# One streaming-encoder layer: the mixers' weight tiles from a written plan, their roundings in emission order, new charges of the emission clock, modulation at another pace

## The chip, the core and the metric

The kernel runs on one core of a Trainium2 chip. The metric is the device time of one execution in microseconds. Engines are named as the profile names them: PE is TensorE (PEld its weight loads), DVE VectorE, ACT ScalarE, POOL GpSimd, SP SyncE, which issues most of the DMAs.

## What is computed

One layer of a hybrid encoder, 512 prompt tokens and 64 sample tokens, model width 2048, all in float32. Cut to what matters:

```python
mod = jax.nn.silu(c) @ w_ada + b_ada                     # modulation: sh1, sc1, g1, sh2, sc2, g2
h = rmsnorm(x, norm1) * (1 + sc1) + sh1
proj = h @ w_in                                          # columns: a_q a_k a_v a_r a_lr | b_q b_k b_v b_g b_beta b_alpha
# group A: gated linear attention, 4 heads (GLA), state 128 x 256
# group B: gated delta rule after a causal convolution, 8 heads (GDN), state 128 x 128
out = concat([o_a, o_b]) @ w_out
x = x + g1 * out
h = rmsnorm(x, norm2) * (1 + sc2) + sh2
f = (silu(causal_dwconv(h @ w_up_gate) + b) * (h @ w_up_val)) @ w_down
y = rmsnorm(x + g2 * f, final_norm)
```

Prompt and sample have a modulation and recurrent states each; the new states are outputs too.

## The kernel before

A GEMM tile is 128 output columns for all 576 tokens, as two halves of 288. Precision is kept by splitting each float32 operand into a rounded part and a rest: ScalarE copies the raw weights (`raw`) to the rounded `wh`, VectorE subtracts and writes the rest `wl`. One product of 128 contraction rows (`mm6`) is six matmuls, three terms for two halves: `wh` by `hh`, `wh` by `hl`, `wl` by `hh` (lines 744 and 746). A weight tile holds 8 such products (512 KB); an input tile of the projection takes two weight tiles.

The stages in order: the head (normalisation, first modulation, and six input tiles, whose results partly go to DRAM as `early`), the mixers, the output projection in two halves (first the contraction over the GDN heads, then over the GLA heads), the FFN up and down, the final norm.

In the mixers PE gets one long stream: `gdn_heads` and `gla_heads` emit the input tiles, and between the products the recurrences of heads that have their inputs are emitted as jobs, written as generators. After each product `tick` advances an emission clock (`now`, 0.795 us a product), lets every short task go one step, lets the first job in the list that can go on take one step, and lets the modulation take steps: a VectorE multiply-add of a 128 x 512 block of `w_ada` into `acc`, 512 of them in all, at `ADA_RATE` steps a tick and only while the clock's VectorE is not more than 1 us behind.

The clock also foresees when a job's result is ready. Every operation of a wrapped engine is charged with a duration (`OP_US`) to that engine's free time and to the job's `chain`; `until` holds the generator back until the clock has reached the chain. Operations that go through the wrappers `tv`, `ta`, `jv`, `ja` are bound to issue in emission order on VectorE and ScalarE. Not bound are the weight roundings: `split` emits the load and both roundings at the start of each weight tile with priority and with `floating` set, so that they issue as far ahead as buffers allow (three buffers for `raw`, three for `wh` and `wl`).

Job operands live in a pool of 29 tiles of 128 x 512 (`_MixPool`). A job asks for room with `room(n)` and waits until `n + SPARE` tiles are free. The sample jobs (`gdn_samples`, `gla_samples`) process all heads' 64 sample tokens at once and run behind the others. Head outputs go to DRAM (`od`), and `load_o` brings them back, alternately through the buffers `xr` and `raw`, and splits them for the output projection; those of the GDN heads before its first half, those of the GLA heads before its second. Small matmuls and transposes of the jobs are issued in the wrappers of lines 2410 and 2414; line 2368 issues job operations of VectorE and ScalarE, line 2395 other wrapped operations.

Of the kernel before, what the change touches and what calls it, by code (L numbers as in the profile page):

```python
# [32 lines left out]
SPARE = 5  # L33
JOB_RATE, ADA_RATE = 1.0, 0.72
# [3 lines left out]
TABLE_US, COLUMN_US = 1.28, 0.06  # L38
# [76 lines left out]
class Kern:  # L115
    def __init__(self, tc, ctx, i, o):
        self.tc, self.nc, self.ctx, self.i, self.o = tc, tc.nc, ctx, i, o
        self.n = 0
        self.cp = ctx.enter_context(tc.tile_pool(name="cp", bufs=1, side="left"))
        self.psum = ctx.enter_context(ExitStack())  # L120
        self.pg = self.psum.enter_context(tc.tile_pool(name="pg", bufs=2, space=PSUM))
        self.c, self.scrap = {}, []
# [91 lines left out]
    def gdn(self, qF, kF, x, gain, hcols, gb, s0, s_out, o_put, last_level, room=None):  # L214
# [15 lines left out]
        nbe, wk, egl = self.g_nbe[:, hcols], self.g_wk[:, hcols], self.g_egl[:, hcols]  # L230
        yield from self.wait_for(x, "q")
        yield from self.wait_for(x, "k")
        back, room = room, room or (yield from self.room(5))
# [5 lines left out]
        A.activation(du, du, AF.Exp, scale=-1.0)  # L239
        for m, op, up in ((du, ALU.is_ge, 1), (dl, ALU.is_gt, -1)):  # L240
            for z, sign in ((slice(0, 2), up), (slice(2, 4), -up)):
                self.pool.affine_select(m[:, z], m[:, z], pattern=[[0, 2], [sign, P]], compare_op=op, fill=0.0, base=0, channel_multiplier=-sign)
        if pair:
            self.pool.memset(du[0:64, 0:2, 64:P], 0.0)
            self.pool.memset(du[64:P, 2:4, 0:64], 0.0)
        A.activation(gb, gb, AF.Exp)
# [13 lines left out]
        V.scalar_tensor_tensor(kt[:, 1], kt[:, 1], -1.0, beta, op0=ALU.mult, op1=ALU.mult)  # L260
        yield from self.until()
# [64 lines left out]
        for b in range(4):  # L326
# [16 lines left out]
            yield from self.hop()  # L343
            for n, (lo, hi, s_) in enumerate(parts):
# [18 lines left out]
            A.activation(ops[:, b], ps[:, :P], AF.Copy, scale=rq[:, at:at + 1])  # L363
# [73 lines left out]

    def timed(self, f, *a):
# [26 lines left out]
    def inverse16(self, a, work, room):  # L465
# [23 lines left out]
        for i in range(1, 15):  # L489
# [3 lines left out]
            V.tensor_tensor(xx[:, rest, :i], xx[:, rest, :i], xt[:, rest, :i], op=ALU.add)  # L493
            if i % 4 == 0:
# [26 lines left out]
    def gla(self, nb, qF, kF, g, x, s0, s_out, o_put, room=None):  # L521
# [12 lines left out]
        back, room = room, room or (yield from self.room(4))  # L534
# [8 lines left out]
        for s in LEVELS:  # L543
# [10 lines left out]
            V.tensor_tensor(qe, asks(g), ref, op=ALU.subtract)  # L554
            A.activation(e, e, AF.Exp, scale=1.0 / 16.0)
# [5 lines left out]
            for r in range(nb // 2):  # L561
# [22 lines left out]
        self.drop(kF, back)  # L584
        egl = self.small(4)
        A.activation(egl[:, :nseg].rearrange("p (h n) -> p h n", h=2), walk(g, seg - 1, (hw - seg + 1, 2), (seg, nseg // 2)),
                     AF.Exp, scale=1.0 / 16.0)
# [12 lines left out]
        for b in range(nb):  # L600
# [7 lines left out]
            if not first:  # L608
                for lo, hi, s_ in parts:
                    T.matmul(ops[lo:hi, b % 2], qd[:, at_b, lo:hi], s_, start=False, stop=True)  # L610
            for n, (lo, hi, s_) in enumerate(parts):
# [12 lines left out]
            A.activation(junk, ops[:, b % 2], AF.Square, scale=1.0 / 16.0, accum_out=ss[:, b:b + 1])  # L624
# [123 lines left out]
    def gemm(self, ps, src, acts, order=None, tick=lambda: None, w=None):  # L748
# [612 lines left out]
    def in_tile(self, off, order=None):  # L1361
        ps = self.pgt()
        self.gemm(ps, self.w_in(off), self.h, order, tick=self.tick)
        return ps

    def slots(self, t):

        v = t.rearrange("p (two r t) -> p two r t", two=2, t=P)
        return v[:, 0], v[:, 1, :, ::-1]

# [23 lines left out]
    def gdn_conv(self, ps, t, dst, name, h, done):  # L1394
# [8 lines left out]
        V.tensor_copy(cb[:, 518:582].rearrange("p (h t) -> p h t", h=2), ps[:, :, HP:HT])  # L1403
        V.tensor_copy(cb[:, 515:518], self.vmap["st_conv"].rearrange("p (i t) -> p t i", i=3)[:, t])
# [31 lines left out]
    def gdn_heads(self):  # L1436
# [3 lines left out]
        def conv_tile(n, off, h, x):  # L1440
            ps = self.ps_q0 if h == 0 and n == 0 else self.in_tile(off + h * P)
# [4 lines left out]
        def qk(h):  # L1446
            x = {}
            q = conv_tile(0, OFF_BQ, h, x)
            if h == 0:
                self.narrow(self.kp)  # L1450
            gb = self.decays(self.gd[4 * h:4 * h + 4])
            k = conv_tile(1, OFF_BK, h, x)
            self.start(self.gdn(q, k, x, self.vec("gdn_norm", 0), slice(4 * h, 4 * h + 4),
                                      gb, None, o["p_gdn"][0, 0, h],
# [3 lines left out]
        def vg(h, x):  # L1458
            conv_tile(2, OFF_BV, h, x)
            ps = self.in_tile(OFF_BG + h * P)  # L1460
# [23 lines left out]
    def gdn_samples(self):  # L1484
# [4 lines left out]
        for name, n in (("v", "v"), ("gate", "g")):  # L1489
# [5 lines left out]
                          self.vec("gdn_norm", 0), slice(32, 36), self.decays(self.gd[32:36], room), _States(self, "state_gdn", P),  # L1495
# [9 lines left out]
    def gla_samples(self, x):  # L1505
# [3 lines left out]
        self.put_ready(x, "g", None, 0.0)  # L1509
        yield from self.gla(2, *tiles, x,  # L1510
# [11 lines left out]
    def gla_gate(self, h, g, done):  # L1522

        V, A, T = self.tv, self.ta, self.jt
        y, gss, ys = self.m(), self.half()[:, :TS], self.half()[:, :TS]
# [24 lines left out]
        done(self.chain + HOP_US)  # L1550

    def gla_heads(self):
# [3 lines left out]
        for h in range(4):  # L1556
            self.ending = h == 3
            qk, x = [], {}
            for name, off, sc in (("aq", OFF_AQ, Q_SCALE), ("ak", OFF_AK, 1.0)):
                if (name, h) in self.early:  # L1560
                    t = self.m()
                    self.nc.sync.dma_start(t, self.early[name, h])
                    qk.append(b4(t))
                    continue
                ps = self.in_tile(off + h * P)
# [4 lines left out]
            g = b4(self.m())  # L1570

            def gated(at, x=x, h=h):
                self.put_ready(x, "g", None, at)
                if h == 3:
                    self.start(self.gla_samples(xs))
            self.spawn(self.gla_gate(h, g.rearrange("p b t -> p (b t)"), gated))
            self.start(self.gla(4, *qk, g, x, None, o["p_gla"][0, 0, h], lambda f, t, h=h: self.put_o(2 * h + f, t)))
            vT = [self.m().rearrange("p (b t) -> p b t", b=2) for _ in range(2)]
            for f in range(2):
                ps = self.in_tile(OFF_AV + h * 256 + f * P)  # L1580
# [4 lines left out]
                def turn(t=t, f=f, vT=vT, x=x, h=h):  # L1585
                    tp = self.transpose4(b4(t))
                    self.drop(t)
                    for b in range(2):
# [6 lines left out]
            for f in range(2):  # L1595

                ps = self.in_tile(OFF_AR + h * 256 + f * P, (8, 0) if h == 3 and f == 1 else None)
# [666 lines left out]
def layer_kernel(tc, i, o):  # L2264
    nc = tc.nc
    with ExitStack() as ctx:
# [18 lines left out]
        with ExitStack() as early:  # L2285
            K.wp = pool(early, "wp", "right", bufs=3)
            with ExitStack() as right:
# [9 lines left out]
                with ExitStack() as st:  # L2297
# [6 lines left out]
                    K.ada = K.ada_blocks(range(8, 24), acc)  # L2304
                    K.gdn_heads()
                    K.gla_heads()

                    w, ob = {}, []
                    for k in range(8, 16):
                        ob.append(K.load_o(k, lambda k=k: K.htiles(k)))  # L2310
                        if k == 11:
                            w[0] = K.wtile(K.w_cols("w_out", 0, 8)(0, 8))
                    K.x1 = []
                    for m in range(KD):
# [3 lines left out]
                        K.gemm(ps, K.w_cols("w_out", m, 8), ob, tick=K.tick, w=w.get(m))  # L2318
# [191 lines left out]
```

## Time and profile before

| | us |
|---|---|
| median of 3 runs | 2729.12 (2728.79 to 2731.55) |
| the profiled execution | 2729.87 |
| its span, first to last instruction | 2728.2 |
| PE busy in the span | 2682.6 (98%) |
| DVE busy | 2292.2 (84%) |
| ACT busy | 1295.6 (47%) |
| POOL busy | 477.8 (18%) |

In the profile's rows a group is named by line, engine, operation and tiles (out<-in). Its busy time and the mean of one follow, then the engine's idle time ahead of it and what ended that. A wait row names who waited for whom, the sum, the number and the longest. Matmuls overlap, so that a busy PE is not a measure of its rate.

### The profile page before, as it was taken

What the parts mean: (1) busy time and instruction counts of PE and PEld (TensorE: products, weight loads), DVE (VectorE), ACT (ScalarE), POOL (GpSimd) and SP (SyncE); (2) the same over time, 40 slices, a digit from 0 to 9 for tenths busy, and PEclk for the clock granted to TensorE, in tenths of its full rate; (3) what the DMA queues carried; (4) which work ended last, traced back from release to release, by engine and by line L of the source; (5) the groups of instructions that cost most, each with busy time, mean ns of one, the idle gap of its engine ahead of it and who ended that gap; (6) DMA issues with size and microseconds to landing.
All of it is one profiled execution on the core that took longest, in us unless ns stands there. A gap on an engine that the chain in (4) does not pass through costs nothing.

```text
span 2728.2 us, 52233 instructions
## 1 busy us (share of the span) xinstructions
PE 2682.6 (98%) x20208; PEld 2620.1 (96%) x20208; DVE 2292.2 (84%) x3747; ACT 1295.6 (47%) x2317; POOL 477.8 (18%) x461
## 2 busy tenths in 40 slices
PE   7999999999999999999999999999999999999998
PEld 5799999999999999999999999999999999999998
DVE  4579899988989895688999999999999976888996
ACT  4246454555554442554545454545454544333453
POOL 0001010110001000001333333333333300000241
PEclk9999999999999999999999999999999999999999
DMA  9986565555565583634555555555555595674762
GB/s 303 347 256 186 151 171 161 168 171 147 154 180 164 159 270 90 179 98 120 162 168 163 167 163 167 165 165 167 163 168 162 165 312 184 197 223 121 237 181 82
DMA packets 646203, 487.84 MB, mean 179 GB/s; under 512 B 66601, under 2 KB 568356, under 8 KB 645956
## 3 DMA queue, kind: packets, MB, share of 16 engines
q1 hardware_dynamic: 632852, 471.04, 57.5%
q10 hardware_dynamic: 13104, 13.47, 1.7%
q8 instruction: 159, 2.61, 0.4%
q14 instruction: 88, 0.72, 0.1%
HBM read 400.38 MB, written 84.04 MB: 178 GB/s over the span
## 4 chain that ended last, share of the span: by engine, by line
PE 82%; DVE 8%; DMA 4%; issue 3%; ACT 2%; SPq 0%; POOL 0%; ACTq 0%; DVEq 0%; POOLq 0%
PE g L744 17%; PE bank L1881 16%; PE bank L1880 16%; PE bank L1882 16%; PE g L746 8%; PE bank L2414 4%; DVE wl L1790 2%; PE bank L744 1%; PE bank L2410 1%; DVE m L2368 1%; DVE wl L2395 1%; DMA raw<-in_w_out_dram 1%; PE bank L973 1%; DMA raw<-in_w_in_dram 1%; DVE slot L2076 1%
## 5 line engine op out<-in xcount | busy, mean ns | idle before, releaser
L1881 PE MATMUL bank<-slot,wh 128*128 128x290 f32 (+1 forms) x3584 | 1067.3, 298 | 0.0
L1880 PE MATMUL bank<-slot,wh 128*128 128x290 f32 (+1 forms) x3584 | 1063.1, 297 | 1.0 <-DVE v L1903 0.6
L1882 PE MATMUL bank<-slot,wl 128*128 128x290 f32 (+1 forms) x3584 | 1060.3, 296 | 1.3 <-DVE wl L1790 1.2
L1882 PEld LDWEIGHTS bank<-slot,wl 128*128 128x128 f32 x3584 | 680.0, 190 | 2.9 <-DVE wl L1790 2.5
L1880 PEld LDWEIGHTS bank<-slot,wh 128*128 128x128 f32 x3584 | 675.4, 188 | 5.2 <-issue 4.4
L1881 PEld LDWEIGHTS bank<-slot,wh 128*128 128x128 f32 x3584 | 677.0, 189 | 0.1
L744 PE MATMUL g<-hh,wh 128*128 128x288 f32 x2048 | 470.1, 310 | 1.6 <-DVE kt L2395 0.7
L1788 ACT ACTIVATE wh<-raw 128x1024 fp32r<-128x1024 f32 (+1 forms) x304 | 280.7, 924 | 348.5 <-PE bank L1881 325.2
L746 PE MATMUL g<-hh,wl 128*128 128x288 f32 x2048 | 442.7, 297 | 2.3 <-DVE wl L1141 2.3
L744 PE MATMUL g<-hl,wh 128*128 128x288 f32 x2048 | 442.8, 297 | 0.3 <-DVE hl L775 0.2
L1790 DVE TENSOR_TENSOR wl<-raw,wh 128x1024 fp32r<-128x1024 f32 (+1 forms) x304 | 374.2, 1231 | 69.0 <-ACT wh L1788 66.0
L1788 ACT ACTIVATE wh<-s 128x1024 fp32r<-128x1024 f32 (+1 forms) x228 | 211.0, 927 | 296.5 <-PE bank L1881 136.6
L744 PEld LDWEIGHTS g<-hh,wh 128*128 128x128 f32 x2048 | 325.5, 189 | 15.9 <-issue 10.4
L746 PEld LDWEIGHTS g<-hh,wl 128*128 128x128 f32 x2048 | 330.8, 189 | 4.2 <-DVE wl L1141 2.7
L744 PEld LDWEIGHTS g<-hl,wh 128*128 128x128 f32 x2048 | 330.6, 189 | 2.7 <-issue 1.9
L1790 DVE TENSOR_TENSOR wl<-s,wh 128x1024 fp32r<-128x1024 f32 (+1 forms) x228 | 251.0, 1102 | 13.7 <-ACT wh L1788 12.5
L2395 ACT ACTIVATE wh<-raw 128x1024 fp32r<-128x1024 f32 x135 | 143.1, 1062 | 185.6 <-PE g L744 145.1
L2004 POOL TENSOR_TENSOR j<-j,j 128x288 f32<-128x288 f32 (+1 forms) x120 | 186.0, 1557 | 84.0 <-ACT j L2008 82.1
L2395 DVE TENSOR_TENSOR wl<-raw,wh 128x1024 fp32r<-128x1024 f32 x135 | 165.9, 1229 | 35.5 <-ACT wh L2395 35.2
L2395 DVE SCALAR_TENSOR_TENSOR acc<-aw,ct,acc 128x512 f32<-128x512 f32 x264 | 187.7, 743 | 0.0
L2395 DVE SCALAR_TENSOR_TENSOR acc<-xr,ct,acc 128x512 f32<-128x512 f32 x216 | 154.2, 748 | 0.0
L2076 DVE TENSOR_TENSOR slot<-bank,slot 128x288 f32<-128x288 f32 x184 | 83.0, 451 | 33.7 <-PE bank L1882 32.6
(317 smaller groups left out, 3269.4 us busy)
## 6 DMA issues: line engine op xcount, KB each, us to landing
raw<-in_w_up_dram SPq DMA_DIRECT2D x176, 512.0 KB
raw<-in_w_in_dram SPq DMA_DIRECT2D x100, 512.0 KB
raw<-in_w_down_dram SPq DMA_DIRECT2D x128, 320.0 KB
slot<-cd SPq DMA_DIRECT2D x140, 288.0 KB
aw<-in_w_ada_dram SPq DMA_DIRECT2D x74, 512.0 KB
cd<-j SPq DMA_DIRECT2D x120, 288.0 KB
xr<-in_w_ada_dram SPq DMA_DIRECT2D x54, 512.0 KB
hraw<-in_w_ada_dram SPq DMA_DIRECT2D x40, 512.0 KB
```

What stands on the lines that cost most here:

```text
L744: T.matmul(ps[:, h if bank is None else bank, :n], wh, x[:, h, :n], start=f, stop=False)
L746: T.matmul(ps[:, h if bank is None else bank, :n], wl, ah[:, h, :n], start=False, stop=stop)
L973: T.matmul(ps[32 * k:32 * k + 32, :w], cs[:, k0 + k], got[n][k // per][:, k % per], start=(n == together - 1 + 8 * g + 4 * (1 - mi)), stop ...
L1788: self.nc.scalar.activation(hi, src, AF.Copy)
L1790: self.nc.vector.tensor_tensor(lo, src, hi.bitcast(F32), op=ALU.subtract)
L1880: T.matmul(ps, wh[:, j], hi, start=(c < 3 and j == 0), stop=False, skip_group_check=True)
L1881: T.matmul(ps, wh[:, j], lo, start=False, stop=False, skip_group_check=True)
L1882: T.matmul(ps, wl[:, j], hi, start=False, stop=(j == n - 1), skip_group_check=True)
L2004: minus = lambda out, a, b: G.tensor_tensor(out, a, b, op=ALU.subtract)
L2076: V.tensor_tensor(dst, ps, dst, op=ALU.add)
L2395: r = f(*a, **kw)
L2414: return self.engine.matmul(out, *a, **kw)
```

## The change

- The mixers' weight tiles come from a list written beforehand (`make_plan`): all 100 weight tiles of the remaining input tiles, then 16 of the output projection's first half. Three loads are issued at once; after that `gemm_planned` issues one load per weight tile.
- The roundings are no longer floating. The ScalarE rounding of the next weight tile is emitted after the second product of the current one (`w_split`), the VectorE rounding once the clock says that the first is done, or after the sixth product (`w_rest`). Both are bound in emission order.
- The clock: `beside` charges an operation that nothing of the job waits for next without lengthening the job's chain; small steps of the 16 x 16 inversion are charged 0.12 us more per pair; waits (`until`) stand ahead of some ScalarE operations.
- Rooms are granted in the order of asking, except that `gla_gate` asks in front and without spare; `SPARE` goes from 5 to 2. Decays, early q and k, the gate and the turned v take their tiles later. `gla_samples` waits until the last GLA head has begun.
- `ADA_RATE` goes from 0.72 to 0.58 steps a tick.

```diff
-SPARE = 5
-JOB_RATE, ADA_RATE = 1.0, 0.72
+SPARE = 2
+JOB_RATE, ADA_RATE = 1.0, 0.58
...
-    def room(self, n):
-        while self.mp.spare() < n + SPARE:
+    def room(self, n, first=False):
+        room = _Room(n)
+        self.asking.insert(0 if first else len(self.asking), room)
+        while self.asking[0] is not room or self.mp.spare() < n + (0 if first else SPARE):
             yield WAIT
+        self.asking.pop(0)
         self.mp.held += n
-        return _Room(n)
+        return room
...
+    @contextmanager
+    def beside(self, at):
+        old, self.chain = self.chain, max(at, self.now)
+        yield
+        self.chain = max(old, self.chain)
...
             V.tensor_tensor(xx[:, rest, :i], xx[:, rest, :i], xt[:, rest, :i], op=ALU.add)
+            self.slower("V", 2 * SMALL_US)
...
-            A.activation(ops[:, b], ps[:, :P], AF.Copy, scale=rq[:, at:at + 1])
+            with self.beside(ready):
+                A.activation(ops[:, b], ps[:, :P], AF.Copy, scale=rq[:, at:at + 1])
...
+    def gemm_planned(self, ps, acts, order):
         n, i = len(acts), 0
-        for k0 in order or range(0, n, 8):
-            k1 = min(n, k0 + 8)
-            wh, wl = w or self.wtile(src(k0, k1))
-            for k in range(k0, k1):
+        for k0 in order:
+            if not self.ready:
+                self.w_split()
+            self.w_rest()
+            wh, wl = self.ready.pop(0)
+            for k in range(k0, k0 + 8):
                 self.mm6(ps, wh[:, k - k0], wl[:, k - k0], acts[k], i == 0, i == n - 1)
-                tick()
+                self.tick()
+                if k == k0 + 1:
+                    self.w_split()
+                    self.w_load()
+                elif self.rest and (self.now >= self.rest[3] + HOP_US or k == k0 + 5):
+                    self.w_rest()
                 i += 1
+    def w_load(self):
+        if self.plan:
+            raw, src = self.raw(), self.plan.pop(0)
+            with self.tc.high_priority(offset=AHEAD):
+                self.nc.sync.dma_start(raw.rearrange("p (k n) -> p k n", k=8), src)
+            self.loaded.append(raw)
+    def w_split(self):
+        if not self.loaded:
+            return
+        raw = self.loaded.pop(0)
+        hi, lo = [self.wq.tile([P, 1024], F32R, tag="w" + c, bufs=3, name=self.name("w" + c)) for c in "hl"]
+        self.ready.append([x.rearrange("p (k n) -> p k n", k=8) for x in (hi, lo)])
+        old, self.chain = self.chain, self.now
+        self.ja.activation(hi, raw, AF.Copy)
+        self.rest, self.chain = (raw, hi, lo, self.chain), old
+    def w_rest(self):
+        if self.rest:
+            raw, hi, lo, at = self.rest
+            old, self.chain, self.rest = self.chain, at, None
+            self.jv.tensor_tensor(lo, raw, hi.bitcast(F32), op=ALU.subtract)
+            self.chain = old
+    def make_plan(self):
+        off = [OFF_BK]
+        for h in range(8):
+            off += [OFF_BQ + (h + 1) * P, OFF_BK + (h + 1) * P] if h < 7 else []
+            off += [OFF_BV + h * P, OFF_BG + h * P]
+        for h in range(4):
+            off += [o + h * P for n, o in (("aq", OFF_AQ), ("ak", OFF_AK)) if (n, h) not in self.early]
+            off += [o + h * 256 + f * P for o in (OFF_AV, OFF_AR) for f in range(2)]
+        self.plan = [self.w_in(o)(k0, k0 + 8) for n, o in enumerate(off) for k0 in ((8, 0) if n == len(off) - 1 else (0, 8))]
+        self.plan += [self.w_cols("w_out", m, 8)(0, 8) for m in range(KD)]
+        self.loaded, self.ready, self.rest = [], [], None
+        for _ in range(3):
+            self.w_load()
...
-    def gla_samples(self, x):
+    def gla_samples(self, x, last):
+        while "begun" not in last:
+            yield WAIT
         room = yield from self.room(7)
...
+                    K.make_plan()
                     K.gdn_heads()
                     K.gla_heads()
-                    w, ob = {}, []
+                    ob = []
                     for k in range(8, 16):
                         ob.append(K.load_o(k, lambda k=k: K.htiles(k)))
-                        if k == 11:
-                            w[0] = K.wtile(K.w_cols("w_out", 0, 8)(0, 8))
...
-                        K.gemm(ps, K.w_cols("w_out", m, 8), ob, tick=K.tick, w=w.get(m))
+                        K.gemm_planned(ps, ob, (0,))
```

More of the change, by code (lines that the diff above doesn't have):

```diff
@@ L230, in gdn @@
         nbe, wk, egl = self.g_nbe[:, hcols], self.g_wk[:, hcols], self.g_egl[:, hcols]
+        back, room = room, room or (yield from self.room(6))
+        gb = self.decays(self.gd[hcols], room)
+        self.moved()
         yield from self.wait_for(x, "q")
         yield from self.wait_for(x, "k")
-        back, room = room, room or (yield from self.room(5))
+        yield from self.until()
         dl, du = self.m4(room), self.m4(room)
@@ L533, in gla @@
         yield from self.wait_for(x, "g")
-        back, room = room, room or (yield from self.room(4))
+        g = x["g"]()
+        kept = [type(t) is tuple for t in (qF, kF)]
+        back, room = room, room or (yield from self.room(3 + sum(kept)))
+        x["begun"] = True
+        if any(kept):
+            qF, kF = [self.get_early(t, room) if type(t) is tuple else t for t in (qF, kF)]
+            self.moved(sum(kept))
+            yield from self.until()
         at = self.m(room)[:, :w].rearrange("p (b t) -> p b t", b=nb)
@@ L554, in gla @@
             V.tensor_tensor(qe, asks(g), ref, op=ALU.subtract)
+            yield from self.until()
             A.activation(e, e, AF.Exp, scale=1.0 / 16.0)
@@ L1587, in turn @@
                     self.drop(t)
+                    if f == 0:
+                        vT += [self.m().rearrange("p (b t) -> p b t", b=2) for _ in range(2)]
                     for b in range(2):
```

100 lines of the change are left out of this document (57 added, 43 removed).

## The prediction

> **What bounds the kernel now.** I read the page first: the span and the share of each engine. Then the busy time by stage, cut where the mixers begin and end.
>
> ```profile
> span 2728.2 us, 52233 instructions
> PE 2682.6 (98%) x20208; PEld 2620.1 (96%) x20208; DVE 2292.2 (84%) x3747; ACT 1295.6 (47%) x2317; POOL 477.8 (18%) x461
> 140.00:960.00 820.00, 813.74 (x6270) 793.06 (x6270) 724.04 (x1578) 419.72 (x1018) 69.47 (x72) 1.00 0.61 173
> 960.00:1101.00 141.00, 138.24 (x1009) 133.53 (x1008) 101.81 (x203) 55.54 (x99) 7.05 (x21) 0.99 0.60 180
> ```
>
> The columns of the last two rows are the stretch, its length, the busy time of PE, weight loads, DVE, ACT and POOL, the granted TensorE clock, the DMA share and GB/s. TensorE is busy 98% of the span. The change touches what is emitted between 140 and 1101 us (input projection, both mixers, first half of the output projection), and there PE stands idle for 6.3 + 2.8 = 9.0 us in all. No matmul is added or removed, so the gain is bounded by stalls of about this size. Next, who ends PE's and the weight loads' waits there (engine, line waited for, us in total, times, longest), and the same for ACT and DVE from 200 to 1000 us:
>
> ```profile
> PE bank L2414 <- DVE m L2368: 3.1, 4, 1.0
> PE bank L2414 <- ACT m L2395: 2.0, 1, 2.0
> PE bank L2414 <- DVE m L2395: 1.7, 3, 1.0
> PE bank L2414 <- DVE sq L2368: 1.4, 2, 0.9
> PE g L744 <- DVE kt L2395: 0.7, 1, 0.7
> PEld bank L2414 <- issue: 7.7, 23, 1.2
> ACT wh L2395 <- PE g L744: 121.2, 53, 6.6
> DVE wl L2395 <- ACT wh L2395: 15.2, 14, 3.5
> ```
>
> All five PE rows, 8.9 us, are waits of or behind the recurrence jobs' small matmuls (bank, line 2414), four of them on VectorE and one on ScalarE. No row has PE waiting for a rounded weight (wl, wh): the GEMM itself is fed in time. The last two rows show what today's roundings do: issued as far ahead as buffers allow, they sit on ScalarE waiting for a buffer that PE still holds, and on VectorE waiting for ScalarE, with job work behind them.
>
> **The change part by part.** Sums are made against the profiled execution's 2729.87 us (span 2728.2 and 1.7 around it), 0.75 above the runs' median of 2729.12.
>
> *Roundings in emission order and the clock's charges.* The 116 weight tiles of the plan (the 100 halves of input tiles in the row below, and 16 of the output projection) keep their one ScalarE and one VectorE rounding each; only the place moves. Now a rounding can land in front of a job operation that a PE matmul needs:
>
> ```profile
> raw<-in_w_in_dram SPq DMA_DIRECT2D x100, 512.0 KB
> 369.33 1.21 DVE L2395 TENSOR_TENSOR wl<-raw,wh 128x1024 fp32r<-128x1024 f32 x1
> ...
> 372.05 1.22 DVE L2395 TENSOR_TENSOR wl<-raw,wh 128x1024 fp32r<-128x1024 f32 x1
> ...
> 375.60 0.34 DVE L2368 SCALAR_TENSOR_TENSOR sq<-bank,kt,m 128x128 f32<-128x128 f32 x1
> 376.09 0.46 PE L2414 MATMUL bank<-sq,m 128*128 128x128 f32 x2 [0.44 <-DVE sq L2368]
> ```
>
> Two roundings, started 2.7 us apart, then a job operation late by 0.44 us. Not every such stall has one before it:
>
> ```profile
> 403.90 2.54 DVE L2395 SCALAR_TENSOR_TENSOR ca<-conv_in,cols,ca 128x579 f32<-128x579 f32 x3 [0.26 <-ACT ca L2395]
> 406.42 1.09 DVE L2395 TENSOR_TENSOR m<-cm,consts 128x128 f32<-128x128 f32 x3
> 407.56 0.71 PE L2414 MATMUL bank<-m,m 128*128 128x128 f32 x4 [0.41 <-DVE m L2395]
> ```
>
> Here only convolution steps stand ahead. The PE rows without the 2.0 on ScalarE and the 0.77 at 964.72 us (both below) make 6.1 us. In order, and charged where it stands, a rounding is foreseen by the emission clock; its prices of convolution and modulation steps stay too low. So I take half gone: −3.1 (bounds: all gone, −6.1; as much again added, +6.1). Of the 7.7 us in which a weight load was late with no releaser shown, most overlaps a running matmul; I take a quarter, −2.0 (bounds −7.7 and 0). New waits for a weight: none in the row list now; at the latest the VectorE rounding is issued after product 6 of 8, and then two products and four matmuls cover it.
>
> ```profile
> 1099.57 0.43 PE L744 MATMUL g<-hh,wh 128*128 128x288 f32 x2
> 1100.38 0.43 PE L744 MATMUL g<-hh,wh 128*128 128x288 f32 x2
> ```
>
> A product takes 0.81 us, so the cover is 2 × 0.81 + 0.54 = 2.2 us for the 1.22 us of a rounding (372.05 above): a VectorE backlog over some 0.9 us makes PE wait. The waits above reach 1.0 us, so that happens sometimes: +1.0 (bounds 0 and the rival below).
>
> *The plan at the turn from the mixers to the output projection.* This is the largest single stall.
>
> ```profile
> 978.26 1.06 ACT L2395 ACTIVATE wh<-raw 128x1024 fp32r<-128x1024 f32 x1 [3.70 <-DMA raw<-in_w_out_dram]
> 979.23 0.62 ACT L2368 ACTIVATE m<-m 128x512 f32<-128x512 f32 x1
> 979.86 1.28 ACT L2395 ACT_TABLE_LOAD   x1
> 981.15 0.60 ACT L2395 ACTIVATE m<-g 128x512 f32<-128x512 f32 x1
> 981.79 0.68 PE L2414 MATMUL bank<-m 128*128 128x128 f32 x4 [1.99 <-ACT m L2395]
> 982.00:984.00 2.00, 2.00 (x15) 2.00 (x15) 2.00 (x6) 1.95 (x4) 0.00 (x0) 0.83 0.91 258
> 984.00:986.00 2.00, 2.00 (x10) 2.00 (x9) 2.00 (x6) 1.26 (x2) 1.14 (x1) 0.50 1.07 324
> 986.00:988.00 2.00, 2.00 (x15) 2.00 (x14) 2.00 (x4) 1.05 (x1) 0.00 (x0) 0.82 1.08 377
> 964.72 0.68 PE L2414 MATMUL bank<-m 128*128 128x128 f32 x4 [0.77 <-DVE m L2368]
> ```
>
> ScalarE waited 3.70 us for the weights of the second output tile, with a job's work behind that rounding; PE then stood 1.99 us, and the clock was at half until 987, which loses 0.34 + 1.00 + 0.36 = 1.70 us. With 0.77 at 964.72 that is 4.46 us. The plan has these weights loaded before the turn, so this wait goes. What takes its place: two of the three raw buffers then hold output weights while the eight head outputs are loaded, four of them through raw. Such a load holds its buffer for 5.2 us:
>
> ```profile
> 1085.43 0.37 SPq L1616 DMA_DIRECT2D raw<-od  x1
> 1089.83 0.76 DVE L1619 TENSOR_TENSOR slot<-raw,slot 128x576 fp32r<-128x576 f32 x1 [0.57 <-ACT slot L1618]
> 954.16 0.32 SPq L1616 DMA_DIRECT2D raw<-od  x1
> 954.58 0.38 SPq L846 DMA_DIRECT2D raw<-in_w_out_dram  x1
> ```
>
> The last two rows show a head output that got its buffer ahead of an output weight that stands behind it in the program, although that weight carries the higher priority. If this holds, the first goes into the free buffer after the last rounding for the input tiles, about 2 us before the turn (ready 3.2 us in), a second buffer joins after the next rounding some 4 us in (ready at 8.4 and 9.2), and the last is ready at 13.6; until then PE has 14 products of two output tiles (11.3 us) and the jobs. I take 2.0 us of new stall: −4.5 + 2.0 = −2.5. Bounds: −4.5; and four loads in series, 20.8 us against those 11.3: +9.5 + 1.7 of clock − 4.5 = +6.7.
>
> [...]
>
> *Loads on SP's queue.*
>
> ```profile
> SPq L846 <- DVE wl L2395: 183.8, 66, 8.8
> ```
>
> A weight load waits for the VectorE rounding of the tile that held its buffer, with the jobs' transfers queued behind it: 183.8 us over 66 waits today. The plan's loads wait for the same kind of rounding, no longer ahead but in order: 0; if it costs a job, PE shows it as a late small matmul, which is in the bound of +6.1.
>
> *Rooms, SPARE, tiles taken later.* Jobs may start earlier. No engine's work changes; the loads of decays and of early q and k, as many as before on SP's queue, only move behind the grant of a room. The jobs' end is hidden:
>
> ```profile
> 1095.46 0.76 DVE L1619 TENSOR_TENSOR slot<-xr,slot 128x576 fp32r<-128x576 f32 x1
> 1101.19 0.69 PE L744 MATMUL g<-slot,wh 128*128 128x288 f32 x4
> ```
>
> The last head output is rounded at 1096.2, PE turns to it at 1101.2: an earlier end earns nothing, one up to 5.0 us later costs nothing, beyond that one to one. 0.
>
> *Modulation at 0.58 a tick.* Today's real pace, and its last steps (durations: least, median, longest; first and last start):
>
> ```profile
> 400.00:500.00 100.00, 1.28 (x16) 0.32 (x16) 46.39 (x68) 0.00 (x0) 1.00 0.60 167
> L2395 DVE SCALAR_TENSOR_TENSOR acc<-aw,ct,acc x264: 709/744/817, 184.8 to 1031.7; 128x512 f32<-128x512 f32 x132
> ```
>
> The third busy time is VectorE's: 68 steps in 100 us. At 0.72 a tick and some 110 ticks in 100 us it would be 79, so the backlog test, not the rate, paces it now. 512 steps at 0.58 end at tick 883 of 928 (800 for the input tiles, 128 for the output tiles), some 20 us after today's 1032, still before 1101. VectorE's sum stays. 0. The clock charges 0.65 us (0.12 + 512/960) for the step that takes 0.744.
>
> Sum: −3.1 − 2.0 + 1.0 − 2.5 + 0 + 0 = −6.6: 2729.87 − 6.6 = 2723.3, 0.21% under the median.
>
> **The rivals.**
> *Stalls only move.* PE takes its matmuls in order, and the clock still charges 0.65 for 0.744 us; the stall at 407.56, with no rounding ahead, speaks for it. Terms near zero: 2729.
> *All goes.* Every PE row, the clock loss and half of the late loads: 8.9 + 1.7 + 3.9 = 14.5: 2715. The dense VectorE (724 of 820 us) speaks against it.
> *The turn starves.* With priority deciding the buffers, the +6.7 case: −3.1 − 2.0 + 1.0 + 6.7 = +2.6: 2732.5.
> *Weights late (the other side).* Today's waits lists show the rounding far ahead; a tile ahead and in strict order, it stands behind every job operation issued before it, some of which wait for PE. It decides from a VectorE backlog of 0.9 us on. One tile in seven late by the 1.0 us of the longest VectorE wait: 17 us instead of 1.0: 2723.3 + 16 = 2739. Against it: the clock holds modulation back above a backlog of 1 us, and the rounding is moved ahead by a priority of its own. [...]
>
> **How the numbers follow.** Forecast case 0.43 (own range 2719 to 2727, three quarters of it beyond 0.2%); all goes 0.12; only move 0.20; the turn starves 0.10 (a third of it beyond 0.2%); weights late 0.15. 0.2% is 5.5 us, about what a measurement of this kernel can tell from none. Faster: 0.32 + 0.12 = 0.44; slower: 0.15 + 0.03, and 0.03 of the only-move case = 0.21; same: 0.35. The range goes from 2715 (all goes) to 2738, just short of the late weights' 2739.
>
> **What would show it.** Right: in the mixers no PE wait on ScalarE near the turn, no half clock there, PE's named waits at some 4 us, ScalarE's 121 us behind PE nearly gone, VectorE's 15 us behind wh likewise. Wrong: PE waiting for wl or wh in the mixers (late weights); PE waiting for hh or hl, or raw<-od issued 5 us apart, at the turn (starved); head outputs rounded after PE's last first-half product (jobs late); PE's named waits again near 9 us (only moved).

## The result

| | before | after |
|---|---|---|
| median of 6 runs each, us | 2728.61 (2725.95 to 2731.55) | 2773.80 (2771.08 to 2776.45) |
| the profiled execution, us | 2729.87 | 2776.45 |
| its span, us | 2728.2 | 2774.7 |

The changed kernel takes 1.0164 times as long (95% interval 1.0154 to 1.0175): slower by 45 us, outside the predicted range. In the changed kernel a GEMM's matmuls have the lines 774 and 776 (744 and 746 before), the roundings of the plan line 2462, the jobs' small matmuls lines 2504 and 2508.

The page first, then busy time in the two stretches that the prediction showed (stretch, length, busy PE, weight loads, DVE, ACT and POOL, granted clock, DMA share, GB/s):

```profile
span 2774.7 us, 52158 instructions
PE 2700.7 (97%) x20208; PEld 2633.8 (95%) x20208; DVE 2296.0 (83%) x3747; ACT 1293.9 (47%) x2319; POOL 471.8 (17%) x461
140.00:960.00 820.00, 792.96 (x6017) 769.47 (x6014) 679.59 (x1500) 408.60 (x1001) 64.20 (x72) 0.98 0.57 161
960.00:1101.00 141.00, 132.98 (x958) 126.69 (x956) 115.67 (x228) 53.33 (x105) 6.42 (x21) 0.99 0.66 196
```

The work is the same: VectorE's sum is 2296.0 against 2292.2, ScalarE's 1293.9 against 1295.6. From 140 to 960 us PE is busy 20.8 us less than before and issues 6017 matmuls instead of 6270, at a clock of 0.98 instead of 1.00. The turn to GLA's half of the output projection (PE's first matmul of slot by wh) moves from 1101.2 to 1148.2. The mixers, counted from the end of the head's narrow matmuls to that turn, take 985.9 us instead of 941.5. The head takes 2.7 us more, what follows the turn the same within 0.6 us. In the thirteen profiles of this document the head's narrow matmuls end anywhere from 159.7 us (before) to 162.6, without any order in what was changed, so these 2.7 us need not come of the change.

Who ends PE's waits from 140 to 1160 us (line waited for, us in total, times, longest), and two rows for ScalarE and VectorE from 200 to 1000 us:

```profile
PE g L776 <- DVE wl L2462: 22.1, 20, 3.2
PE g L774 <- ACT wh L2462: 9.0, 4, 4.3
PE bank L1367 <- DVE na L1356: 3.1, 1, 3.1
PE bank L2508 <- DVE sl L2462: 0.8, 1, 0.8
PE g L774 <- ACT hh L1713: 0.8, 1, 0.8
PE bank L2508 <- DVE m L2489: 0.8, 1, 0.8
PEld bank L2508 <- issue: 4.7, 17, 1.0
ACT m L2462 <- PE bank L2504: 93.0, 31, 12.9
DVE m L2462 <- PE bank L2508: 42.7, 57, 4.4
```

The waits on jobs, which the change was about, are down from 8.9 us to 1.6 (the sl and m rows). In their place PE waits 31.1 us for rounded weights, 22.1 of it for VectorE's half. ScalarE's roundings no longer wait for a buffer that PE holds (121.2 us before), and VectorE waits 0.6 us for wh (15.2 before). Both engines now wait for PE, since the jobs' operations head their queues. With every row, PE waits 36.6 us in the mixers instead of 8.9: 27.7 more. The granted clock is at half in six stretches there (three of 3.4 us, two of 6.8 and one of 10.2), which together lose 17.0 us of full-speed time (half of the time at half clock, 1.7 us for each 3.4); before, one lost 1.7. 27.7 of waits, 15.3 of clock and 2.7 in the head are 45.7 of the 46.5 us that the span grew. That is a little too much: 2.6 us of the clock's loss fall on time in which PE stood anyway, so some 3 us of the 46.5 have no row here.

One such stall. VectorE from 503 to 514 us (start, length, instructions joined), PE's next matmul, and the windows around it:

```profile
503.16 1.21 DVE L2462 TENSOR_TENSOR wl<-raw,wh 128x1024 fp32r<-128x1024 f32 x1
504.29 2.53 DVE L2489 SCALAR_TENSOR_TENSOR ca<-conv_in,cols,ca 128x579 f32<-128x579 f32 x3
...
506.80 3.76 DVE L2462 TENSOR_TENSOR m<-m 48x50 f32<-48x50 f32 x16
...
510.60 0.82 DVE L2462 TENSOR_TENSOR m<-m 48x26 f32<-48x26 f32 x4
511.46 1.08 DVE L2462 COPY m<-m 16x256 f32<-16x256 f32 x3
512.57 1.23 DVE L2462 TENSOR_TENSOR wl<-raw,wh 128x1024 fp32r<-128x1024 f32 x1
513.85 0.53 PE L776 MATMUL g<-hh,wl 128*128 128x288 f32 x2 [2.32 <-DVE wl L2462]
512.00:514.00 2.00, 0.15 (x1) 0.15 (x2) 1.73 (x3) 2.00 (x10) 1.40 (x1) 1.00 0.15 33
514.00:516.00 2.00, 2.00 (x13) 2.00 (x14) 0.37 (x3) 2.00 (x9) 1.15 (x4) 0.79 0.41 91
516.00:518.00 2.00, 2.00 (x10) 2.00 (x9) 2.00 (x4) 2.00 (x6) 0.00 (x0) 0.50 1.26 294
```

VectorE does not rest: between two roundings stand 8.2 us of convolution steps, the small steps of 16 x 16 inversions and copies, and a tile of eight products lasts 8 × 0.81 = 6.5 us. The rounding comes as soon as its turn does, PE has stood 2.32 us, and then the clock falls to half. The matmuls of the next product by the same `wh` start only behind the late one, at 514.22: PE takes its matmuls in order.

The costliest stretch ahead of the turn, from 443 us on, has both halves. ScalarE and VectorE ahead of it, and PE:

```profile
440.05 1.28 ACT L2462 ACT_TABLE_LOAD   x1
441.34 1.68 ACT L2462 ACTIVATE m<-m 128x512 f32<-128x512 f32 x3
...
445.40 1.11 ACT L2462 ACTIVATE wh<-raw 128x1024 fp32r<-128x1024 f32 x1
446.56 0.61 PE L774 MATMUL g<-hh,wh 128*128 128x288 f32 x2 [3.28 <-ACT wh L2462]
447.30 1.08 DVE L2489 TENSOR_TENSOR m<-cm,consts 128x128 f32<-128x128 f32 x3
448.31 2.73 DVE L2489 SCALAR_TENSOR_TENSOR acc<-xr,ct,acc 128x512 f32<-128x512 f32 x4
450.96 1.40 DVE L2489 SCALAR_TENSOR_TENSOR acc<-aw,ct,acc 128x512 f32<-128x512 f32 x2
452.28 1.21 DVE L2462 TENSOR_TENSOR wl<-raw,wh 128x1024 fp32r<-128x1024 f32 x1
453.55 0.85 PE L776 MATMUL g<-hh,wl 128*128 128x288 f32 x2 [3.17 <-DVE wl L2462]
```

Ahead of `wh` ScalarE works through a job's operations, a table load and exponentials among them; ahead of `wl` VectorE has three operations that put the 16 x 16 inverses in their places (out of `cm`) and six modulation steps, although wh was there from 446.5.

At the turn to the output projection (ScalarE, PE, and the head outputs' loads on SP):

```profile
1017.28 1.45 ACT L1713 ACTIVATE hh<-xr 128x576 fp32r<-128x576 f32 x2 [2.24 <-DMA xr<-od]
1018.75 1.28 ACT L2489 ACT_TABLE_LOAD   x1
...
1020.77 1.28 ACT L2462 ACT_TABLE_LOAD   x1
1022.07 0.42 ACT L2462 ACTIVATE m<-m 128x256 f32<-128x256 f32 x1
1022.39 1.04 ACT L2462 ACTIVATE wh<-raw 128x1024 fp32r<-128x1024 f32 x1
1023.49 0.66 PE L774 MATMUL g<-hh,wh 128*128 128x288 f32 x2 [4.29 <-ACT wh L2462]
1016.61 0.33 SPq L1711 DMA_DIRECT2D raw<-od  x1
1024.83 0.33 SPq L1711 DMA_DIRECT2D raw<-od  x1
1027.62 0.32 SPq L1711 DMA_DIRECT2D raw<-od  x1
1030.71 0.33 SPq L1711 DMA_DIRECT2D raw<-od  x1
```

The old wait there, a rounding that waited for its weights, is gone. The new rounding has its weights but stands behind a split that waits 2.24 us for a head output, and behind two table loads: 4.29 us.

### The profile page after: what moved, and what is told of

The parts are those of the page before. It is cut to its first block, busy times and chain, and to the rows that moved or that the text cites. A ratio compares the mean times of both kernels' runs of the same rounds, so it can differ in the third digit from the quotient of the medians.

```text
span 2774.7 us, 52158 instructions
## 1 busy us (share of the span) xinstructions
PE 2700.7 (97%) x20208; PEld 2633.8 (95%) x20208; DVE 2296.0 (83%) x3747; ACT 1293.9 (47%) x2319; POOL 471.8 (17%) x461
## 4 chain that ended last, share of the span: by engine, by line
PE 67%; DVE 6%; DMA 1%; ACT 1%; issue 1%; ACTq 0%; POOL 0%; DVEq 0%; SPq 0%
PE bank L1976 16%; PE bank L1975 16%; PE bank L1977 16%; PE g L774 9%; PE g L776 5%; PE bank L2508 2%; DVE wl L1885 2%; PE bank L774 1%; DVE acc L2489 1%; DVE slot L2171 1%; DVE wl L2462 1%; PE bank L776 1%; PE bank L2504 1%; DMA aw<-in_w_ada_dram 1%; DVE s L1896 0%
## 5 line engine op out<-in xcount | busy, mean ns | idle before, releaser
L776 PE MATMUL g<-hh,wl 128*128 128x288 f32 x2048 | 446.9, 300 | 24.5 <-DVE wl L2462 22.1
L1885 DVE TENSOR_TENSOR wl<-s,wh 128x1024 fp32r<-128x1024 f32 (+1 forms) x228 | 250.8, 1102 | 13.6 <-ACT wh L1883 12.5
L2489 DVE SCALAR_TENSOR_TENSOR acc<-aw,ct,acc 128x512 f32<-128x512 f32 x276 | 197.2, 744 | 4.8 <-DMA aw<-in_w_ada_dram 4.8
L2489 DVE SCALAR_TENSOR_TENSOR acc<-xr,ct,acc 128x512 f32<-128x512 f32 x204 | 145.9, 747 | 0.0
L2462 DVE TENSOR_TENSOR wl<-raw,wh 128x1024 fp32r<-128x1024 f32 x116 | 141.4, 1219 | 2.0 <-ACT wh L2462 1.8
L2462 ACT ACTIVATE wh<-raw 128x1024 fp32r<-128x1024 f32 x116 | 122.7, 1059 | 16.2 <-PE g L774 14.3
```

Source lines behind the costliest of these rows:

```text
L776: T.matmul(ps[:, h if bank is None else bank, :n], wl, ah[:, h, :n], start=False, stop=stop)
L1885: self.nc.vector.tensor_tensor(lo, src, hi.bitcast(F32), op=ALU.subtract)
L2462: return f(*a, **kw)
L2489: r = f(*a, **kw)
```

## The experiments

The theory after the comparison (A): a rounding bound in emission order, one tile ahead, stands behind whatever burst of job operations was emitted before it, and a burst longer than a tile's lead stops PE. The rivals: the plan's loads hold the raw buffers too long (B); or rooms, clock charges and the modulation's pace crowd VectorE and ScalarE (C).

All kernels are the changed one with the edit shown, except where it says before. The last columns are, in the mixers of the profiled execution, their length, PE's waits for wl and wh, all of PE's named waits, and the clock's loss (1.7 us for each 3.4 at half).

| kernel | median, us | against before (95%) | mixers | weights | all waits | clock |
|---|---|---|---|---|---|---|
| before | 2728.6 | | 941.5 | 0 | 8.9 | 1.7 |
| after | 2773.8 | 1.0164 (1.0154 to 1.0175) | 985.9 | 31.1 | 36.6 | 17.0 |
| both roundings free | 2733.3 | 1.0013 (1.0003 to 1.0022) | 944.4 | 0 | 7.0 | 0 |
| two tiles ahead | 2732.1 | 1.0011 (1.0001 to 1.0020) | 943.1 | 0.8 | 8.8 | 6.8 |
| no plan, no binding | 2730.0 | 1.0006 (0.9997 to 1.0016) | 941.5 | 0.9 | 5.7 | 0 |
| VectorE's rounding free | 2764.8 | 1.0126 (1.0106 to 1.0146) | 975.4 | 14.0 | 23.7 | 17.0 |
| ScalarE's rounding free | 2777.0 | 1.0167 (1.0146 to 1.0188) | 989.4 | 27.0 | 37.1 | 20.4 |
| VectorE's right behind | 2768.5 | 1.0139 (1.0120 to 1.0159) | 976.2 | 24.3 | 32.0 | 13.6 |
| after, pace 0.72 | 2786.4 | 1.0210 (1.0190 to 1.0230) | 1004.3 | 30.6 | 43.5 | 27.2 |
| both free, pace 0.72 | 2737.2 | 1.0028 (1.0018 to 1.0038) | 950.1 | 0 | 6.9 | 5.1 |
| before, pace 0.58 | 2730.8 | 1.0006 (0.9998 to 1.0015) | 941.5 | 2.7 | 10.6 | 0 |
| two ahead, SPARE 5 | 2737.0 | 1.0028 (1.0017 to 1.0039) | 949.5 | 0.9 | 11.7 | 8.5 |
| two ahead, first two free | 2737.1 | 1.0035 (1.0021 to 1.0048) | 949.5 | 5.4 | 11.6 | 5.1 |

**Both roundings free of the order.** Plan, loads, rooms, clock and pace stay.

```diff
 def w_split(self):
...
-    old, self.chain = self.chain, self.now
-    self.ja.activation(hi, raw, AF.Copy)
-    self.rest, self.chain = (raw, hi, lo, self.chain), old
+    with self.tc.high_priority(offset=AHEAD):
+        self.floating = True
+        self.ta.activation(hi, raw, AF.Copy)
+        self.tv.tensor_tensor(lo, raw, hi.bitcast(F32), op=ALU.subtract)
+        self.floating = False
```

> The changed kernel, plan, clock, rooms and modulation as they are; only the roundings of the planned weight tiles are issued unbound again (both emitted where the ScalarE one stood, free to run ahead of the jobs' operations). Theory A (a rounding bound in emission order stands behind bursts of job operations that are longer than the cover of one tile): PE's waits for wl and wh in the mixers (22.1 + 9.0 us) fall under 3 us, no half clock in mid-stage, 2722 to 2734 us. Theory B (the plan's loads, three raw buffers held ahead, bring the weights late): stays at 2765 to 2775, PE still waiting for wh and wl. Theory C (rooms, clock and modulation pace crowd VectorE): 2755 to 2775, PE waiting for job operations or weights.

Measured 2733.25. Its waits of PE (the two longest rows of eight) and of ScalarE, and its first stretch:

```profile
PE bank L2510 <- DVE m L2464: 1.8, 1, 1.8
PE bank L2510 <- ACT ts L2491: 1.7, 1, 1.7
ACT wh L2491 <- PE g L774: 99.2, 53, 5.8
140.00:960.00 820.00, 812.77 (x6219) 788.60 (x6217) 710.70 (x1569) 426.62 (x1036) 64.36 (x74) 1.00 0.58 168
```

No wait for wl or wh is left, the clock stays at 1.00, and ScalarE's roundings wait 99.2 us for PE again, as they did before. Some 40 of the 45 us hang on where the two roundings issue, so the plan's loads (B) and the crowding (C) explain at most the last 5. The edit does a little more than unbind: VectorE's half is emitted earlier and both get the priority of the loads. The next experiment keeps the binding.

**In order, but two tiles ahead.**

```diff
-            if not self.ready:
-                self.w_split()
+            while len(self.ready) < 2 and self.loaded:
+                self.w_rest()
+                self.w_split()
+                if len(self.ready) == 2:
+                    self.w_load()
```

> The changed kernel with the roundings still bound in emission order, but two weight tiles ahead instead of one. Theory A: a tile is about 8 us, the longest PE waits for wl and wh were 3.2 and 4.3 us, so a second tile of cover takes nearly all of them: 2725 to 2742 us, PE's waits for wl and wh under 5 us. Theory B: the loads are a tile nearer to their rounding, so worse or the same: 2770 to 2790. Theory C: 2760 to 2775.

Measured 2732.06. VectorE in this kernel at the same work as at 503 us in the changed one, and PE's waits for weights:

```profile
483.33 1.21 DVE L2465 TENSOR_TENSOR wl<-raw,wh 128x1024 fp32r<-128x1024 f32 x1
484.46 2.52 DVE L2492 SCALAR_TENSOR_TENSOR ca<-conv_in,cols,ca 128x579 f32<-128x579 f32 x3
...
491.28 1.23 DVE L2465 TENSOR_TENSOR wl<-raw,wh 128x1024 fp32r<-128x1024 f32 x1
PE g L776 <- DVE wl L2465: 0.8, 2, 0.5
```

The burst is still there, though shorter (6.7 us from the end of one rounding to the start of the next, 8.2 at 503 us), and PE does not notice. Longer ones pass too: the roundings at 456 and 468 us start 12.6 us apart, and the second is still 7.6 us ahead of its matmul. So it is not the order as such but the lead. From the traces I paired each plan tile's VectorE rounding with PE's first matmul that uses it (94 tiles, from the plan's fourth to its 97th; the k-th rounding with the k-th sixteen matmuls by wl) and took the time from the end of the one to the start of the other; the last column is from the start of one rounding to the start of the next:

| lead, us | least | a tenth below | median | longest time between two roundings |
|---|---|---|---|---|
| before | 0.6 | 6.7 | 13.2 | 21.5 |
| after | 0.1 | 0.1 | 1.6 | 19.8 |
| both free | 4.3 | 9.0 | 12.8 | 17.4 |
| two ahead | 0.1 | 5.2 | 9.3 | 15.4 |
| VectorE's free | 0.1 | 1.1 | 4.2 | 16.9 |
| ScalarE's free | 0.1 | 0.1 | 1.5 | 20.6 |

The roundings come as unevenly in every kernel of the table: of 93 spacings, 54 to 58 are over 7.5 us (before, some of them while ScalarE waited for a buffer). In the kernel before one stretch, the 21.5 us up to the rounding at 367.60, left 0.6 of the usual 13.2 us of lead, and PE did not stop; ScalarE's half too came late there, at 361.29, with no idle time on ScalarE before it. The change left a lead of 1.6 in the median.

**One half free at a time.** For the first, `self.floating = True` and `False` around VectorE's subtraction in `w_rest`; for the second, around ScalarE's copy in `w_split`.

> The changed kernel with the VectorE rounding (wl) issued unbound, the ScalarE rounding (wh) still bound in emission order. Theory A says which queue holds the weights back: most of the 22.1 us of waits for wl come from VectorE bursts (convolution and inversion steps ahead of it at 504 to 513 us), the 9.0 us for wh from ScalarE bursts. So wl waits fall to those that follow a late wh: 2742 to 2756 us, wh waits still 7 to 12 us. If the ScalarE rounding is what comes late in most cases (rival A2), little changes: 2762 to 2775.

> The other half alone: ScalarE rounding unbound, VectorE rounding bound and one tile ahead. Theory A: waits for wh go (under 1.5 us), waits for wl stay at 12 to 20 us: 2748 to 2764 us. Rival A2 (ScalarE is the late one): 2730 to 2740.

Measured 2764.83 and 2777.03: both missed, the first by 9, the second by 13. The rival A2, that ScalarE's half is the late one, has the first in its range and is refuted by the second (2730 to 2740 expected). PE's waits, of the kernel with VectorE's half free and then of that with ScalarE's:

```profile
PE g L774 <- ACT wh L2464: 9.0, 6, 2.7
PE g L776 <- DVE wl L2464: 5.0, 6, 2.1
```
```profile
PE g L776 <- DVE wl L2464: 27.0, 15, 3.9
```

I had taken the two halves to share the loss. They do not add: a free VectorE rounding still can't start before ScalarE's `wh`, which is bound (VectorE waits 19.6 us for it from 200 to 1000 us, against 0.6), and a free ScalarE rounding leaves `wl` where it was. Either binding keeps most of the loss, and only both freed together give it back. With VectorE's half free the mixers are 33.9 us longer than before; the rows show 14.8 of waits and 15.3 of clock, of which 14.0 are waits for weights. What the clock lost follows stalls of several kinds there, so how much of it belongs to the weights is open.

**VectorE's rounding emitted right behind ScalarE's**, instead of up to four products later:

```diff
                 if k == k0 + 1:
                     self.w_split()
+                    self.w_rest()
```

> The changed kernel, both roundings bound and one tile ahead, but the VectorE rounding is emitted right behind the ScalarE one (after the second product) instead of when the clock says that the first is done (third to sixth product), so its cover grows by one to four products, 0.8 to 3.2 us, while VectorE may now stand waiting for ScalarE. Theory A: part of the wl waits goes, wh waits stay: 2750 to 2765 us. If VectorE's waiting for ScalarE costs more than the cover gains: 2775 to 2790.

Measured 2768.45, 3 us above what was expected. Waits for wl fall from 22.1 to 15.1 us, but now VectorE stands waiting for ScalarE's half, with job work behind it (22.5 us from 200 to 1000 us, against 0.6): the late emission of the second half was some 6 us of the 45, not their cause.

**The rest of the change without plan and binding**: the old split per weight tile, all else kept.

```diff
-            if not self.ready:
-                self.w_split()
-            self.w_rest()
-            wh, wl = self.ready.pop(0)
+            src = self.plan.pop(0)
+            wh, wl = w or self.wtile(src)
...
+                        if k == 11:
+                            w[0] = K.wtile(K.w_cols("w_out", 0, 8)(0, 8))
...
```

> The changed kernel without the plan's loads ahead and without the bound roundings: each weight tile is loaded and rounded unbound from its own start, as in the kernel before; clock charges, rooms, spare of 2 and modulation at 0.58 stay. Theory A and B alike: the loss goes, 2718 to 2732 us; what the rest is worth shows against the kernel before, and I expect -3 to -8 us from the turn and the named job waits. Theory C: 2755 or more.

Measured 2729.95, the same as before; the gain of 3 to 8 did not come. PE's named waits are 3.2 us shorter and the 1.7 of clock is saved, but the mixers take 941.5 us as before. What grew is the time from one small job matmul to the next when they follow each other: 138.3 us over 1183 pairs, 133.9 over 1161 before. The 22 pairs more make some 2.5 of these 4.4 us (at 0.115 us a pair), and stand in place of pairs with a GEMM's matmul; why a pair also takes a little longer, 0.117 us, stays open.

**The modulation's pace.** Three kernels: the changed one with `ADA_RATE` back at 0.72, the one with both roundings free likewise, and the kernel before with 0.58.

> The changed kernel with the modulation back at 0.72 steps a tick. Theory A: the bursts ahead of the late roundings are job operations, which the rate does not touch; modulation fills VectorE somewhat more: 2770 to 2785 us. Theory C (the pace of the modulation crowds or frees VectorE at the wrong time): a change of over 15 us either way, 2755 or less, or 2790 or more.

> The kernel with both roundings free of emission order, and 0.72 modulation steps a tick in place of 0.58. My theory, that the pace hurts only through what stands ahead of a bound rounding: without the bound it costs nothing, so as with 0.58, 2733 (2730 to 2736), no PE wait for wl or wh in the mixers. Rival, that a denser VectorE in itself makes PE wait, whatever the roundings: some of the +12.6 that the pace cost with bound roundings shows, 2738 to 2746.

> The kernel before, with 0.58 modulation steps a tick in place of 0.72. As the prediction had it, the pace is worth nothing by itself: 2728.3 (within 2). Rival, that a thinner VectorE takes some of the 6.1 us of PE waits on jobs: 2722 to 2726. Other rival, that the later end of the modulation costs at the turn: 2731 to 2735.

Measured 2786.36, 2737.17 and 2730.76; the first two lie 1 us above their ranges, the third half a us. Each set against the runs of before beside it, the faster pace costs 11.5 us with bound roundings (56.6 above before, not 45.2) and 3.2 with free ones (8.2, not 5.0; the two ratios' intervals still overlap), and the slower pace gains the kernel before nothing. So the price of a denser VectorE is larger where the roundings are bound. That it is paid through the roundings themselves is not shown: in the profile at 0.72 PE's waits for wl and wh are no longer than at 0.58 (30.6 and 31.1 us), while its waits on jobs grow (from 1.6 us to 8.5) and the clock loses 27.2 us instead of 17.0. The theory's "no price at all with free roundings" was 1 us too low in its upper end, and the rival's 2738 was not reached.

**Looking for a version that beats both.** Two tiles ahead with `SPARE` back at 5, and two tiles ahead with the plan's first two tiles rounded free of the order (in `make_plan`, as in the first experiment).

> Bound roundings two tiles ahead, and SPARE back at 5 from 2. If earlier rooms (SPARE 2) crowd VectorE and ScalarE and so cost what is left over the kernel before: 2726 to 2729. If rooms are worth nothing, as the prediction had it: 2732 (2730 to 2734). If jobs that start later pile up at the turn: 2736 and more.

> Roundings in order and two tiles ahead, and the first two tiles of the plan rounded free of the order, during the head's last matmuls. Two tiles ahead alone still had a PE wait of 2.8 us behind na at 173 us, with 3.4 us of clock behind it. Theory: there the first bound roundings, held until the first convolution has been emitted, land on the head's end; free, that wait and its clock go: 6 us off 2732, so 2726 (2723 to 2728), a tie with the kernel before or just under it. Rival, that the wait on na comes from the head's own copies, whatever the roundings: 2732 (2730 to 2734).

Measured 2736.95 and 2737.07, 5 us above two tiles ahead. The first is in the range given for jobs that pile up at the turn, but around the turn, from 980 to 990 us, PE waits 4.4 us, no more than two tiles ahead alone (4.7), so the cause is not shown. The second missed both of its ranges. It did what it was meant to: with two tiles ahead PE waited 2.8 us for `na` at 173 us with 3.4 of clock behind, and that is gone. But its longest waits are now these:

```profile
PE g L776 <- DVE wl L2475: 3.6, 3, 2.9
PE g L774 <- ACT hh L1726: 2.1, 1, 2.1
PE g L774 <- ACT wh L2475: 1.8, 1, 1.8
```

At 257 and 260 us wh and then wl are late by 1.75 and 2.91 us, with 3.4 of clock. It looks as if all that is emitted later had shifted, so that a burst fell where a rounding was due; no run tried that. No kernel here beats the one before.

## Why the prediction was wrong

By its own terms (us, against before; the clock's losses put beside the stall that stands ahead of them):

| term | predicted | measured |
|---|---|---|
| waits on jobs | −3.1 | −4.5 (6.1 to 1.6) |
| late weight loads | −2.0 | −3.0 (7.7 to 4.7), mostly beside running matmuls |
| the turn | −2.5 | +2.3 (4.29 + 0.78 + 1.7 of clock for 4.46) |
| new waits for a weight | +1.0 | +26.8, and 8.5 of clock |
| `na` at the mixers' begin | not foreseen | +3.1, and 3.4 of clock |
| half clock from 194.3 us on | not foreseen | 3.4, with no wait of PE's in the 16 us before it |
| the head | 0 | +2.7 |

The wait for `na` is a price of the binding too: it is there, 2.8 to 3.4 us long, in the six kernels here whose first ScalarE roundings are bound, and in none of the other seven.

*The step that failed* is "New waits for a weight", and with it the dismissal of "weights late". The prediction set a cover of 2.2 us, from the sixth product on, against the VectorE waits of up to 1.0 us that PE had shown. But those 1.0 us were what job matmuls lacked; what a bound rounding meets is the whole queue emitted ahead of it, whether anyone waits for that or not. The trace of before could tell how much it takes: roundings up to 21.5 us apart, and a lead that fell from 13.2 us in the median to 0.6 at the least. The new lead had to be held against that, not against a wait. And only VectorE was looked at: ScalarE's half was given no wait at all and measured 9.0, 4.3 of it at the turn.

The direction was there as a rival, with the right mechanism (strict order behind operations of which some wait for PE), but at 17 us for one tile in seven late by 1.0. Measured are 24 waits over 116 tiles, about one for every five, by 1.3 us in the mean, and a third as much again by the clock (10.2 us with the turn's 1.7), which the rival did not price. Neither reason against it held. The clock is meant to hold modulation back above a backlog of 1 us, but six modulation steps ran ahead of the rounding at 452.28. The priority of its own doesn't help a rounding that is bound behind the last operation emitted. In the trace VectorE is busy without a break from the rounding at 503.16 until the next at 512.57, with 8.2 us of job operations between the two.

*Right* were the bound (no engine's work changed), the waits on jobs, the end of ScalarE's 121.2 us behind PE and of VectorE's 15.2 behind wh, and the end of the wait for weights at the turn. *The turn* itself came out about midway between the −2.5 and the +6.7 of the rival "the turn starves": the loads of head outputs through raw went 8.2, 2.8 and 3.1 us apart, but PE stood for `wh`, behind a split that waited for one of them, and only 0.78 us for `hh`. *Rooms and SP's queue at 0* agree with the kernel without plan and binding, the same as before; with two tiles ahead, though, `SPARE` at 5 instead of 2 came out 5 us longer. *Modulation at 0*: the pace gains nothing by itself, but its end was put at 1052, and came later:

```profile
L2489 DVE SCALAR_TENSOR_TENSOR acc<-aw,ct,acc x276: 712/744/887, 185.4 to 1122.6; 128x512 f32<-128x512 f32 x138
```

1122.6 is still before the turn at 1148.2, and no wait of PE's names `acc`. In the kernel before at 0.58 the last step starts at 1067.7, so some 16 us of the delay are the pace's own; the rest comes with the slower stage.

What stays open: the 2.7 us of the head, the 2 to 5 us by which the repaired kernels stand above the one before, the half clock from 194.3 us on, and how the 35 us with VectorE's half free divide. A kernel of before with the plan alone was not tried.

## What to carry to other kernels

An operation that feeds the bounding engine may be put in program order behind other work only if its lead, in us, is longer than what the longest burst ahead of it takes away, which is the operation's longest spacing less its usual one (941.5 us for 116 tiles, 8.1 us). Two tiles ahead, a spacing of 15.4 us takes some 7 of a lead of 9.3; one tile ahead, 19.8 us take some 12 of a lead of 1.6. Read both from that operation's spacing in the trace and from how far its lead falls, not from the waits that show today, because today's stock hides them. Where two engines prepare an operand one after the other, binding either of them can cost most of what binding both costs (35 and 47 us here, against 45). In this kernel edits that took out a stall of a few us gained nothing in the whole (no plan and no binding, first two free), so such a gain should be forecast near zero.

## What the runs showed of the hardware

Six of the seven PE stalls over 2 us in the mixers of the changed kernel come with half clock, and what it costs doesn't follow from the stall's length alone. PE stalls of 2.08 us (at 646.81) and 2.32 us (at 513.85) each lost 1.7 us of full speed behind them; one of 4.29 us (at 1023.49) also 1.7; 3.28 and 3.17 us, 7 us apart, together 5.1; 3.09 us at 173.97 lost 3.4; and 2.47 us at 260.48 nothing. All losses in the mixers of these profiles come in steps of 1.7 us (in the changed kernel half clock lasts 3.4, 6.8 or 10.2 us). A stall isn't even needed: from 194.3 us on the clock is at half for 6.8 us, and PE's last wait before that, of 0.15 us or more, ended at 178.16; what stands just ahead is a run of small matmuls, 2 and 16 columns wide, at 190.8 to 193.4 us. The same run in the kernel before, at 192.1 to 194.9, was not followed by half clock. In the changed kernel the seven stalls over 2 us, 20.7 us together, have 13.6 us of clock behind them, the shorter ones, 15.9 us together, none that began with them. That is no limit, though: in the kernel before a stall of 1.99 us (at 981.79) has 1.7 behind it, and at the pace of 0.72 one of 1.39 us (at 385.11) too. What the clock costs was only read from the granted clock; no run held it fixed.
